# Three of the four pieces of the first x loaded from ScalarE's queue, and eight products of zeros ahead of the first stage

## The chip, the cores and the metric

The kernel runs on one core of a Trainium2 chip. The time is device microseconds of one execution: before the change 606.63 us, the median of 3 runs (606.6 to 607.01).

## The reference

Two layers of a hybrid block over one sequence of 256 tokens, width 1024, all in fp32. Per layer:

- `h = rms_norm(x, g)`, then one projection `h @ w_in` into the parts of three mixers (an mLSTM in chunks of 64, a block attention "MoBA" and a latent attention "MLA").
- MLA takes two latents, `rms_norm(cq, g_cq) @ w_uq` and `rms_norm(ckv, g_ckv) @ w_ukv`, normalises the heads, **rotates** part of queries and keys by `cos` and `sin` of position times frequency, and does causal softmax attention. MoBA rotates its queries and keys as well.
- `x = x + mix @ w_out`, and `x = x + square(relu(rms_norm(x) @ w_up)) @ w_down`.

## The kernel before

Products in fp32 accuracy are made of three passes: `mm3` (L232 to L235) multiplies high by high, high by low and low by high parts. ScalarE makes the high part of a weight piece (`wh`, L207), VectorE the low part (`wl`, L208), up to six pieces ahead of the one TensorE works on. The weights come in order of use as transfers of up to 1 MB on SyncE's queue (`load`, L188), into three rotating buffers `raw`.

The first stage of layer 0 is different, so that it can start early: `do_lat` multiplies the transposed x (`xts`, four pieces of 256 KB, L250) by the first weights (four pieces, L188) in plain fp32 (L547). VectorE scales `xts` in place by the norm's gain (L508) before that, and ScalarE and VectorE split it into `xh` and `xl` (L511, L512) for all later products.

GpSimd makes the tables of cosines and sines for the rotations (`make_trig`, L302 to L342: a chain of some 40 small steps on `tr`, each of which needs the one before; then the tables `tpq`, `tpk`, `tlq`, `tlk`, L421 to L425). The chain starts from the positions (`psi`) and the first 28 columns of the constants (`ck`), both loaded from ScalarE's queue (L246, L247). Outside this chain GpSimd has a few short steps: `gqk` (L629, a product of gains, which reads columns 57 on of the parameters `par`, the second of two transfers, L257), and three casts of the masks and of the identity (L269 to L272), which read the large part of `ck` (L258). VectorE's first use of a table is `rq` (L438, a rotation of MLA's queries).

The order on each engine is set by a scheduler when the kernel is built, from its own estimate of when each step can start; on the chip every engine then takes its list strictly in order. The transfers take eight counters in turn (DMAHW0 to DMAHW7 in the lists below): a transfer is issued only when the one eight places earlier, which had the same counter, has landed.

Of the kernel before, what the change touches and what calls it, by code (L numbers as in the profile page):

```python
# [12 lines left out]
BF16 = mybir.dt.bfloat16  # L13
# [12 lines left out]
DMA_AHEAD = 2  # L26
SPLIT_AHEAD = 6
LAG = 2

ORDERS = [o.split() for o in ("""  # L30
    lat norm q lat lat lat lat q q qout uq uq ukv tables lss p p mla mla qk p p mla mla moba qk rb
# [40 lines left out]
def load_plan(l):  # L72
# [14 lines left out]
    plan = [seq[i:i + 2] for i in range(0, len(seq), 2)]  # L87
    for j in range(16 + LAG):
        if j < 16:
            plan.append([("up", 2 * j), ("up", 2 * j + 1)])  # L90
        if j >= LAG:
            plan.append([("dn", j - LAG)])
    return plan
# [45 lines left out]
def hybrid_kernel(ctx: ExitStack, tc: tile.TileContext, x: bass.AP, xt: bass.AP, pos: bass.AP,  # L139
                  cst: bass.AP, par: bass.AP, wts: bass.AP, out: bass.AP):  # L140
    nc = tc.nc
    V, A, G, T = nc.vector, nc.scalar, nc.gpsimd, nc.tensor
# [7 lines left out]
    def sb(shape, name, dt=F32, bufs=1, tag=None):  # L150
        return tp.tile([128] + list(shape), dt, name=name, tag=tag or name, bufs=bufs)
# [7 lines left out]
    def sm(shape, name):  # L159
        return ps.tile([128] + list(shape), F32, name=name, tag="sm", bufs=4)  # L160
# [74 lines left out]
        T.matmul(o, lh, rl, start=False, stop=stop, **kw)  # L235


    xts = sb([KT, S], "xts", tag="mix")
    warm = cp.tile([128, 1], F32, name="warm")
    G.memset(warm, 0.0)  # L240
# [6 lines left out]
    nc.scalar.dma_start(ck[:, :K_ID], cst[:, :K_ID])  # L247
    first = load(0, 4)
    for k in range(0, KT, 2):
        nc.sync.dma_start(xts[:, k:k + 2], xt[:, k:k + 2])  # L250
        if k == 0:
            nc.sync.dma_start(pr[0][:, :P_CW], par[0, :, :P_CW])
        next(first)
# [246 lines left out]
    for l in range(L):  # L500
# [472 lines left out]

        for j in range(16 + LAG):
            if j < 16:
# [27 lines left out]
                hs[j] = (hh, hlo)  # L1003
            i = j - LAG
            if 0 <= i < SEVEN:
# [99 lines left out]
```

## Time and profile before

| | |
|---|---|
| median of 3 runs | 606.63 us |
| the profiled execution | 606.65 us |
| its span, first to last instruction | 604.9 us |
| TensorE busy | 592.9 us, 98% |
| VectorE busy | 529.3 us, 88% |
| ScalarE busy | 400.9 us, 66% |
| GpSimd busy | 39.7 us, 7% |
| weights and inputs read | 104.71 MB |

Of the span, 1.75 us less than the execution's time, TensorE is idle for 12 us. GpSimd is busy almost only in the first 38 us. In the profile PE is TensorE's products, PEld its weight loads, DVE VectorE, ACT ScalarE, POOL GpSimd and SP SyncE; a step's idle time stands in square brackets with what ended it.

### The profile page before, as it was taken

To read this page: it belongs to the slowest core of one execution; us is meant where nothing else is said; L and a number is where in the kernel's file an instruction comes from. 1 tells how busy PE (TensorE), PEld (TensorE's weight loads), DVE (VectorE), ACT (ScalarE), POOL (GpSimd) and SP (SyncE) were. 2 spreads that over 40 slices of the span, in tenths; PEclk is the share of its full clock that TensorE was granted. 3 is DMA by queue.
4 is the path that set the end of the run, shared out by engine and by line. 5 is a ranking of instruction groups with operands and counts; after the bars stand their busy time and mean duration, and the time that the engine had idled before them with its cause. 6 is when DMAs were issued, how large, how long until landed. Compare 5 with 4: busy or idle time off the path is not lost.

```text
span 604.9 us, 9950 instructions
## 1 busy us (share of the span) xinstructions
PE 592.9 (98%) x3766; PEld 532.5 (88%) x3766; DVE 529.3 (88%) x967; ACT 400.9 (66%) x655; POOL 39.7 (7%) x91
## 2 busy tenths in 40 slices
PE   5999999999999999999999999999999999999997
PEld 4988978889899999989789897888999899999985
DVE  4889886788999999999987997785899999999995
ACT  4776785556776675766766787564676677575770
POOL 7862000000000000000000000000000000000000
PEclk9999999999999999999999999999999999999999
DMA  8785322443554555545637623326446555555521
GB/s 287 292 308 206 134 75 72 168 148 132 209 198 164 202 204 208 201 171 196 244 109 251 237 89 120 106 70 209 139 140 209 186 192 187 202 209 191 196 102 70
DMA packets 17328, 106.39 MB, mean 176 GB/s; under 512 B 2304, under 2 KB 2816, under 8 KB 5504
## 3 DMA queue, kind: packets, MB, share of 16 engines
q1 hardware_dynamic: 16992, 105.75, 50.1%
q8 instruction: 29, 0.48, 0.3%
q14 instruction: 19, 0.16, 0.1%
q10 hardware_dynamic: 288, 0.02, 0.0%
HBM read 104.71 MB, written 1.05 MB: 175 GB/s over the span
## 4 chain that ended last, share of the span: by engine, by line
PE 75%; DVE 14%; POOL 5%; issue 4%; ACT 2%; DVEq 0%; ACTq 0%; POOLq 0%
DVE wl L208 8%; PE up L233 7%; PE up L234 7%; PE up L235 7%; PE P L233 6%; PE P L234 6%; PE P L235 6%; PE acc L235 2%; PE acc L233 2%; PE acc L234 2%; ACT wh L207 1%; PE vp L234 1%; PE op L233 1%; PE vp L233 1%; PE vp L235 1%
## 5 line engine op out<-in xcount | busy, mean ns | idle before, releaser
L208 DVE TENSOR_TENSOR wl<-raw,wh 128x1024 fp32r<-128x1024 f32 (+2 forms) x196 | 217.6, 1129 | 30.6 <-ACT wh L207 26.6
L207 ACT ACTIVATE wh<-raw 128x1024 fp32r<-128x1024 f32 (+2 forms) x196 | 187.5, 979 | 60.6 <-PE acc L234 18.7
L233 PE MATMUL up<-xh,wh 128*128 128x256 f32 x480 | 135.8, 283 | 0.0
L234 PE MATMUL up<-xh,wl 128*128 128x256 f32 x480 | 135.8, 283 | 0.0
L235 PE MATMUL up<-xl,wh 128*128 128x256 f32 x480 | 135.8, 283 | 0.0
L233 PEld LDWEIGHTS up<-xh,wh 128*128 128x128 f32 x480 | 91.9, 192 | 1.5 <-issue 0.4
L234 PEld LDWEIGHTS up<-xh,wl 128*128 128x128 f32 x480 | 92.0, 192 | 1.1
L235 PEld LDWEIGHTS up<-xl,wh 128*128 128x128 f32 x480 | 92.0, 192 | 0.0
L233 PE MATMUL P<-wh,hrh 128*128 128x512 f32 x228 | 89.5, 393 | 0.3 <-DVE xs L970 0.3
L234 PE MATMUL P<-wh,hrl 128*128 128x512 f32 x228 | 89.3, 392 | 0.0
L235 PE MATMUL P<-wl,hrh 128*128 128x512 f32 x228 | 89.0, 390 | 0.0
L208 DVE TENSOR_TENSOR wl<-tsum,wh 128x1024 fp32r<-128x1024 f32 x56 | 66.3, 1222 | 6.1 <-ACT wh L207 6.1
L1001 ACT ACTIVATE hrh<-us 128x896 fp32r<-128x896 f32 (+1 forms) x32 | 29.2, 912 | 56.9 <-DVE us L996 56.8
L207 ACT ACTIVATE wh<-tsum 128x1024 fp32r<-128x1024 f32 x56 | 56.4, 1050 | 14.2 <-DVE tsum L223 14.2
L235 PEld LDWEIGHTS P<-wl,hrh 128*128 128x128 f32 x228 | 42.8, 188 | 9.5
L233 PEld LDWEIGHTS P<-wh,hrh 128*128 128x128 f32 x228 | 42.9, 188 | 9.1 <-DVE xs L970 0.7
L234 PEld LDWEIGHTS P<-wh,hrl 128*128 128x128 f32 x228 | 42.9, 188 | 8.1
L1002 DVE TENSOR_TENSOR hrl<-us,hrh 128x896 fp32r<-128x896 f32 (+1 forms) x32 | 33.2, 1036 | 4.1 <-ACT hrh L1001 4.1
L221 DVE SCALAR_TENSOR_TENSOR tsum<-raw 128x1024 f32<-128x1024 f32 x28 | 34.1, 1218 | 0.0
L991 ACT ACTIVATE rr<-up 128x512 f32<-128x512 f32 x32 | 18.9, 591 | 18.9 <-PE up L235 18.7
L233 PE MATMUL acc<-wh,mh 128*128 128x512 f32 x64 | 25.6, 399 | 0.0
L235 PE MATMUL acc<-wl,mh 128*128 128x512 f32 x64 | 25.0, 390 | 0.0
(366 smaller groups left out, 1100.4 us busy)
## 6 DMA issues: line engine op xcount, KB each, us to landing
raw<-in_wts_dram SPq DMA_DIRECT2D x91, 1024.0 KB, 4.8
raw<-in_wts_dram SPq DMA_DIRECT2D x2, 740.0 KB, 5.9
raw<-in_wts_dram SPq DMA_DIRECT2D x2, 576.0 KB, 5.2
xts<-in_xt_dram SPq DMA_DIRECT2D x4, 256.0 KB, 4.5
raw<-in_wts_dram SPq DMA_DIRECT2D x4, 256.0 KB, 5.2
xs<-in_x_dram SPq DMA_DIRECT2D x1, 1024.0 KB, 10.2
raw<-in_wts_dram SPq DMA_DIRECT2D x2, 512.0 KB, 3.5
raw<-in_wts_dram SPq DMA_DIRECT2D x2, 478.0 KB, 7.3
```

The source lines that it names most:

```text
L207: A.activation(h[:, :n], r, AF.Copy)
L208: V.tensor_sub(lo[:, :n], r, h[:, :n].bitcast(F32))
L221: V.scalar_tensor_tensor(t[:, :1024], r[:, :1024], -1.0, r[:, 512:1536], op0=OP.mult, op1=OP.subtract)
L233: T.matmul(o, lh, rh, start=start, stop=False, **kw)
L234: T.matmul(o, ll, rh, start=False, stop=False, **kw)
L235: T.matmul(o, lh, rl, start=False, stop=stop, **kw)
L991: A.activation(r, up, AF.Relu)
L1001: A.activation(hh, src, AF.Copy)
L1002: V.tensor_sub(hlo, src, hh.bitcast(F32))
```

## The change

Ahead of everything else GpSimd clears a buffer `zero` of 640 bf16 columns, and TensorE multiplies it by itself eight times into a PSUM buffer that nobody reads. The pieces 2 to 4 of `xts` are issued from ScalarE's queue instead of SyncE's. In the changed kernel lines up to L236 stand one number higher, those after it seven.

```diff
+WARM = 8
...
+    zero = sb([640], "zero", BF16, tag="scr", bufs=2)
+    G.memset(zero, 0.0)
+    idle = sm([512], "idle")
+    for i in range(WARM):
+        T.matmul(idle, zero[:, :128], zero[:, 128:], start=i == 0, stop=i == WARM - 1)
     xts = sb([KT, S], "xts", tag="mix")
...
     for k in range(0, KT, 2):
-        nc.sync.dma_start(xts[:, k:k + 2], xt[:, k:k + 2])
+        (nc.scalar if k else nc.sync).dma_start(xts[:, k:k + 2], xt[:, k:k + 2])
         if k == 0:
             nc.sync.dma_start(pr[0][:, :P_CW], par[0, :, :P_CW])
         next(first)
```

The scheduler answers with another order on several engines. GpSimd, from the scaling of the angles by 1/pi (L320, L327 after the change) on. Before:

```order
L320 TENSOR_SCALAR tr<-tr 128x48 [waits Pool_49]
L315 TENSOR_SCALAR tr<-tr 128x48 [waits Pool_49]
L316 TENSOR_TENSOR tr<-tr 128x48 [waits Pool_49]
...
L315 TENSOR_SCALAR tr<-tr 128x96 [waits Pool_49]
L316 TENSOR_TENSOR tr<-tr 128x96 [waits Pool_49]
L629 TENSOR_TENSOR gqk<-par_74 128x2 [waits DMAHW5_49]
...
L332 TENSOR_SCALAR tr<-tr 128x96 [waits Pool_49]
L269 CAST identb<-ck 128x128 [waits DMAHW6_49]
```

And now:

```order
L327 TENSOR_SCALAR tr<-tr 128x48 [waits Pool_49]
L636 TENSOR_TENSOR gqk<-par_85 128x2 [waits DMAHW5_49]
L322 TENSOR_SCALAR tr<-tr 128x48 [waits Pool_49]
L638 MEMSET gqk 16x1 [waits Pool_49] x2
L638 MEMSET gqk 32x1
L323 TENSOR_TENSOR tr<-tr 128x48 [waits Pool_49]
...
L322 TENSOR_SCALAR tr<-tr 128x48 [waits Pool_49]
L276 CAST identb<-ck 128x128 [waits DMAHW6_49]
L278 CAST mk<-ck 128x128
L279 CAST mk<-ck 128x128
L323 TENSOR_TENSOR tr<-tr 128x48 [waits Pool_49]
```

`gqk`, which waits for the second transfer of `par`, stood behind 17 more instructions of the list and now stands right behind the scaling; the casts, which wait for the large part of `ck`, stood some 25 rows behind it and now stand after five more steps of the chain.

SyncE's queue at the start. Before:

```order
L188 DMA raw<-in_wts_dram 128x512 [waits DMAHW2_49]
L188 DMA raw<-in_wts_dram 128x956 [waits DMAHW3_49]
L188 DMA raw<-in_wts_dram 128x956 [waits DMAHW4_49]
L257 DMA par_74<-in_par_dram 128x136 [waits DMAHW5_49]
L258 DMA ck<-in_cst_dram 128x512 [waits DMAHW6_49]
```

And now:

```order
L189 DMA raw<-in_wts_dram 128x512 x3
L189 DMA raw<-in_wts_dram 128x512 [waits DMAHW1_49]
L189 DMA raw<-in_wts_dram 128x956 [waits DMAHW3_49]
L189 DMA raw<-in_wts_dram 128x956 [waits DMAHW4_49]
L264 DMA par_85<-in_par_dram 128x136 [waits DMAHW5_49]
L265 DMA ck<-in_cst_dram 128x512 [waits DMAHW6_49]
```

The first three weight pieces now follow each other; the transfers of `par` and `ck` stand behind the same weights as before. On ScalarE's queue the pieces 2 to 4 of `xts` come behind the first load of `ck`, the third waiting for `psi` to land and the fourth for that part of `ck`. VectorE's list is the same up to `rq`, apart from the place of some 128x2 and 128x256 steps.

## Rows read from the trace of the kernel before

**Rows 1.** The page: busy time, and the chain that ended last.

```profile
PE 592.9 (98%) x3766; PEld 532.5 (88%) x3766; DVE 529.3 (88%) x967; ACT 400.9 (66%) x655; POOL 39.7 (7%) x91
...
PE 75%; DVE 14%; POOL 5%; issue 4%; ACT 2%; DVEq 0%; ACTq 0%; POOLq 0%
```

**Rows 2.** Waits of TensorE, whole span: us in total, times, longest us.

```profile
PE latp L547 <- DVE xts L508: 5.3, 1, 5.3
PE ltp L706 <- DVE lkl L695: 1.2, 1, 1.2
PE qp L235 <- DVE wl L208: 0.8, 1, 0.8
PE P L233 <- DVE xs L970: 0.3, 1, 0.3
```

**Rows 3.** The chain in order of time, 0 to 60 us: start, us, what.

```profile
36.83 0.21 POOL tlqs L424
...
37.30 0.94 DVE ssl L673
...
57.42 0.61 DVE lkl L695
58.08 1.08 PE ltp L706 x8
```

**Rows 4.** GpSimd's instructions in order: start, us, what.

```profile
4.32 0.18 POOL L302 CAST posf<-psi 128x2 f32<-128x2 int32 x1 [1.76 <-DMA psi<-in_pos_dram]
...
5.76 0.50 POOL L320 TENSOR_SCALAR tr<-tr 128x48 f32<-128x48 f32 x1
...
14.03 1.16 POOL L315 TENSOR_SCALAR tr<-tr 128x96 f32<-128x96 f32 x1
...
17.62 0.20 POOL L629 TENSOR_TENSOR gqk<-par 128x2 f32<-128x2 f32 x1
...
23.18 0.45 POOL L332 TENSOR_SCALAR tr<-tr 128x96 f32<-128x96 f32 x1
...
23.71 0.39 POOL L333 TENSOR_TENSOR tr<-tr 128x96 f32<-128x96 f32 x1
...
30.26 1.35 POOL L339 TENSOR_TENSOR tr<-tr 128x96 f32<-128x96 f32 x1
...
36.78 0.24 POOL L424 TENSOR_TENSOR tlqs<-trig,par 128x32 f32<-128x32 f32 x1
```

**Rows 5.** VectorE's instructions in order.

```profile
30.20 2.50 DVE L208 TENSOR_TENSOR wl<-raw,wh 128x1024 fp32r<-128x1024 f32 x2
...
32.99 2.56 DVE L208 TENSOR_TENSOR wl<-raw,wh 128x1024 fp32r<-128x1024 f32 x2
37.06 0.32 DVE L438 TENSOR_TENSOR rq<-lql,tlqs 128x128 f32<-128x128 f32 x1 [1.50 <-POOL tlqs L424]
...
38.29 2.34 DVE L208 TENSOR_TENSOR wl<-raw,wh 128x1024 fp32r<-128x1024 f32 x2
```

**Rows 6.** SyncE's queue: issue of the second transfer of par.

```profile
6.67 0.65 SPq L257 DMA_DIRECT2D par<-in_par_dram  x1
```

**Rows 7.** Transfers issued in the first 12 us: count, KB each, us to landing.

```profile
xts<-in_xt_dram SPq DMA_DIRECT2D x4, 256.0 KB, 4.5
raw<-in_wts_dram SPq DMA_DIRECT2D x4, 256.0 KB, 5.2
...
raw<-in_wts_dram SPq DMA_DIRECT2D x2, 478.0 KB, 7.3
...
par<-in_par_dram SPq DMA_DIRECT2D x1, 68.0 KB, 7.4
```

**Rows 8.** By stretch: PE, PEld, DVE, ACT, POOL busy, clock, DMA share, GB/s.

```profile
12.00:14.00 2.00, 2.00 (x11) 1.61 (x9) 1.59 (x2) 1.40 (x3) 1.77 (x3) 1.00 1.08 431
```

**Rows 9.** TensorE's products into latp by stretch: busy (count), clock, DMA share, GB/s.

```profile
5.29:8.28 2.99, 2.99 (x7) 1.00 0.91 270
8.28:13.58 5.30, 5.30 (x26) 1.00 1.01 381
```

**Rows 10.** TensorE: first product with the low half of the third p piece.

```profile
42.87 0.39 PE L235 MATMUL pp<-wl,xh 128*128 128x512 f32 x1
```

## The prediction

> **What bounds the kernel now.** I read the page first. TensorE is busy 98% of the span and the chain that ended last runs over it for 75%, but GpSimd, busy 7% of the span, holds 5% of that chain [rows 1]. An engine with so little work on the path must sit in one place, so I read where TensorE waits at all: 5.3 us at the start for the first scaled x, 0.8 us for a low half `wl`, and 1.2 us in one wait of the product `ltp` on `lkl` of VectorE [rows 2]. The chain in order of time says what is behind the last: the table `tlqs` on GpSimd until 37.04, then VectorE without a break from 37.30 to 58.03, then TensorE [rows 3]. The lists of the two engines confirm it: VectorE had finished its split at 35.55 and stood 1.50 us before `rq` until GpSimd's `tlqs` was written at 37.02 [rows 4, 5]. So until 58 us the path is not TensorE. It is the chain of GpSimd from the positions (4.32 us) to `tlqs`, and after it a full VectorE. From 58 us on the path is TensorE, which has no wait of over 0.3 us left. Whatever delays `tlqs` therefore delays the end by the same time; whatever makes the first stage earlier ends in the 1.2 us before `ltp`, which become longer.
>
> **The products of zeros.** Clearing `zero` comes first on GpSimd, but GpSimd waited 1.76 us for the positions anyway [rows 4], and half a microsecond of clearing fits in. The eight products are of 512 columns. TensorE's nearest product of 512 columns took 0.39 us [rows 10]; at that duration end to end they take 3.1 us, at twice that 6.3. They may start once the clearing ends, some 1.3 us into the span, and then end between 4.4 and 7.6, against a first stage at 5.29. At the late end they would delay the first stage by 2.3 us, at the early end by nothing; since the durations overlap between neighbours, I take nothing.
>
> They may also make the first stage faster. In it seven products took 2.99 us, 0.427 each, and the next 26 took 5.30, 0.204 each: half the pace and the full one, the levels of 1.2 and 2.4 GHz [rows 9]. The granted clock column reads 1.00 in both, so the pace tells it, not the column. If all ran at the faster pace, the stage would be shorter by 7 x 0.22 = 1.5 us, as far as its data are there. Of that I count nothing: the next products wait for `wl` (0.8 us of [rows 2]), and everything up to 58 us is behind GpSimd.
>
> **The transfers.** SyncE's queue loses three issues, and the weight pieces go out up to a microsecond earlier. The total in front of the second transfer of `par` stays 4 x 256 + 4 x 256 + 2 x 478 KB, with itself 3072 KB or 3.15 MB [rows 7]. Before it was issued at 6.67 and landed 7.4 us later, at 14.07 [rows 6, 7]. At the best pace of the start, 431 GB/s [rows 8], the same bytes take 7.3 us; if they flowed so from 2.5 us on, `par` would land at 9.8. So it lands between 9.8 and 14.07. I take 13.5, near the late end, because the queue held the same bytes at nearly the same times before. The Trainium skill (DMA: Bandwidth & Descriptors, "Issuing engines are not separate DMA queues") says that transfers from several engines run on the same 16 DMA engines and that a second issuer saves only the time of issuing. By that rule the landing stays near 14; a second queue that brought its own bandwidth would move it to 9.8. On ScalarE's queue the third piece of x now waits for the positions (4.3 us), the fourth for the first part of `ck`; behind them stands ScalarE's split of x, which needs these pieces anyway. I count nothing.
>
> **GpSimd's new order.** This is the term that decides. `gqk` stood at 17.62 us and found `par` landed [rows 4]. Now it comes directly behind the scaling that ended at 6.26 (5.76 + 0.50), and it waits for `par` at 13.5. Behind it in the same list stands the whole rest of the chain, which doesn't need `par` until the tables. The casts follow and wait for the large part of `ck`, issued right behind `par`; the five steps and the small clears between them take about 2 us, so that `ck` should have landed by then.
>
> The stall is 13.5 - 6.26 = 7.2 us. Not all of it arrives at `tlqs`, because GpSimd's pace depends on VectorE. A step of 96 columns takes 0.39 to 0.45 us alone and 1.35 us beside VectorE's split [rows 4, 5]. Up to 35.55 VectorE has the same splits as before, so I let GpSimd advance as it did then from 14.03 on: by 35.5 it had done 32 entries of its list, and 32 entries from `gqk` on end in front of the last polynomial steps (L340 now). Twenty remain up to `tlqs`: 12 of the chain at 0.50 us (0.42 with a gap of 0.08), 6.0 us, and 8 of tables at 0.2, 1.6 us. VectorE stands still in that time, so nothing slows them. That gives 35.5 + 7.6 = 43.1 instead of 37.02, 6.1 us later. The bounds: with `par` at 9.8 and the delay passed on unchanged 3.6 us, with 14.07 and passed on in full 7.8 us. I keep 6.1, since the two stretches of rows it rests on are read at both paces.
>
> **What VectorE and TensorE do then.** Behind `rq` in VectorE's list stand two splits that in the profile began at 38.29; everything there moves by 6.1. TensorE runs ahead on split pieces until 42.87, where it needs the `wl` of the first of these two [rows 10], in the profile written at 39.5, now at 45.6: a wait of some 2.7 us. Then it works on to `ltp`, arrives near 59.6 and waits until 58.08 + 6.1 = 64.2, some 4.6 us. The two are 7.3 us in place of 1.2, and the difference is the delay again. No later wait of TensorE is long enough to give any of it back [rows 2].
>
> After such a wait TensorE may start at the slow pace. The wait of 1.2 us was followed by eight `ltp` products in 1.08 us, no sign of slowness [rows 3]; the wait of 5.3 us at the start was followed by 1.5 us of loss [rows 2, 9]. So the bounds are 0 and 1.5 us. The length of 4.6 us is nearer to the latter, but work in pieces between other engines' steps hides part of a slow pace; I take 0.5. The Trainium skill (TensorE: Matmul & The Clock Gate, "What's actually happening") says that the slow level is the default and that activity lifts it, which speaks for the full 1.5 us; by it the sum would be 614.3.
>
> **The sum.** The profiled execution took 606.65 us, 0.02 above the median, so I add to it: 606.65 + 6.1 + 0.5 = 613.2 us.
>
> **The rivals.**
> - *The early `par`.* The steadier queue brings `par` at 9.8 us, and the delay is 3.6 us: 610.2 us. For it: the mean pace from 5.29 to 8.28 was only 270 GB/s [rows 9], so there is room. Against it: the same bytes by the same 16 engines. Chance 0.12.
> - *Nothing on the path.* `par` is there when GpSimd comes to `gqk`, or the delay stays in VectorE's slack; `tlqs` stays at 37.0 and both edits are hidden. The time is 606.6. For it: `gqk` never waited in the profile. Against it: it came 11 us later then, and VectorE had no slack, since it waited for `tlqs` already. It decides only if `par` lands before 6.3. Chance 0.10.
> - *The first stage counts.* The stage that is up to 1.5 us shorter passes its gain to the end, which needs a GpSimd chain that isn't late and a VectorE that is early: 605.3 us, faster than before. For it: TensorE has 98%. Against it: the chain of [rows 3]. Chance 0.05.
> - *All of it.* The delay passes on in full, 7.8 us, and TensorE restarts slowly, 1.5 us: 615.9 us. For it: GpSimd's steps that ran in VectorE's pauses may now meet its splits. Against it: the last third of the chain runs alone. Chance 0.11.
>
> **How the numbers follow.** My forecast, a delay of 5 to 7 us with up to 1.5 us of slow restart, has 0.62, and its own range is 611.5 to 615. The range of 609.3 to 615.5 takes in the early `par` and part of the last rival, and leaves out the cases with no delay and the extreme, 2 in 10. A measurement of this kernel can tell 0.2%, or 1.2 us, from no change. Faster by more than that is the third rival and little of it: 0.05. No change is the second, with 0.09. Slower holds the rest, 0.86.
>
> **What would show it.** GpSimd idle in front of `gqk` for 6 to 8 us, put down to the transfer of `par`; its steps after 35.5 us at 0.4 us each. VectorE's wait at `rq` of some 7.5 us in place of 1.50, until about 43. TensorE waiting at `pp` and for 4 to 5 us at `ltp`, and the rest of the trace the same but later. The first stage at the fast pace from its start, with no gain at 58 us. I am wrong if GpSimd doesn't wait at `gqk`, or if VectorE reaches `rq` late for another reason, or if TensorE gets its pieces through the stall and the end moves by less than the wait at `rq` grew.

## The result, and the profile after

The changed kernel takes 614.51 us (median of 4 runs, 614.34 to 615.05) against 606.77 us (606.6 to 607.01) in the same comparison: ratio 1.0127, 95% interval 1.0112 to 1.0142. It is 7.7 us slower. The profiled execution took 614.35 us with a span of 612.3; before it was 606.65 with 604.9.

The chain of work that ended last tells the story in its first 14 us (start, us, what):

```profile
2.10 4.46 DMA raw<-in_wts_dram
6.57 6.48 DMA par<-in_par_dram
13.12 0.88 POOL gqk L636
14.01 1.36 POOL tr L322
```

The second transfer of `par` is now itself on the path. It was issued at 6.57 and landed 6.48 us later, at 13.05, and GpSimd, with its whole chain of tables behind `gqk`, stood until then. GpSimd's instructions after the change, to be held against [rows 4]; the time in square brackets is the idle time before the step and what ended it:

```profile
4.49 0.18 POOL L309 CAST posf<-psi 128x2 f32<-128x2 int32 x1 [1.36 <-DMA psi<-in_pos_dram]
...
5.93 0.45 POOL L327 TENSOR_SCALAR tr<-tr 128x48 f32<-128x48 f32 x1
13.12 0.88 POOL L636 TENSOR_TENSOR gqk<-par 128x2 f32<-128x2 f32 x1 [6.75 <-DMA par<-in_par_dram]
...
18.63 1.31 POOL L278 CAST mk<-ck 128x128 bf16<-128x128 f32 x1
...
31.52 2.29 POOL L340 TENSOR_TENSOR tr<-tr 128x96 f32<-128x96 f32 x1
...
35.78 1.30 POOL L339 TENSOR_SCALAR tr<-tr 128x96 f32<-128x96 f32 x1
37.17 0.39 POOL L340 TENSOR_TENSOR tr<-tr 128x96 f32<-128x96 f32 x1
...
43.78 0.24 POOL L431 TENSOR_TENSOR tlqs<-trig,par 128x32 f32<-128x32 f32 x1
```

The scaling ends at 6.38, `gqk` begins at 13.12, and `tlqs` at 43.78 instead of 36.78: a stall of 6.75 us has become a delay of 7.0 us. The casts of the masks found `ck` landed and cost no wait, but two of them ran beside a split of VectorE and took 1.3 us each. VectorE, against [rows 5]:

```profile
9.73 0.61 DVE L515 TENSOR_SCALAR xts<-xts,par 128x256 f32<-128x256 f32 x2 [3.17 <-DMA xts<-in_xt_dram]
12.20 0.62 DVE L515 TENSOR_SCALAR xts<-xts,par 128x256 f32<-128x256 f32 x2 [1.86 <-DMA xts<-in_xt_dram]
...
34.22 2.56 DVE L209 TENSOR_TENSOR wl<-raw,wh 128x1024 fp32r<-128x1024 f32 x2 [0.17 <-ACT wh L208]
44.05 0.32 DVE L445 TENSOR_TENSOR rq<-lql,tlqs 128x128 f32<-128x128 f32 x1 [7.27 <-POOL tlqs L431]
```

Two things stand here. The wait in front of `rq` is 7.27 us where it was 1.50, and `rq` begins at 44.05 where it began at 37.06: 6.99 later. And the third and fourth piece of x, scaled at 8.83 and 10.07 before, were scaled at 9.73 and 12.20; with them all of VectorE's splits moved, the last one in front of `rq` from 32.99 to 34.22. The two pieces as they were scaled before, and their issues before:

```profile
8.83 0.82 DVE L508 TENSOR_SCALAR xts<-xts,par 128x256 f32<-128x256 f32 x2 [2.38 <-DMA xts<-in_xt_dram]
10.07 0.62 DVE L508 TENSOR_SCALAR xts<-xts,par 128x256 f32<-128x256 f32 x2 [0.42 <-DMA xts<-in_xt_dram]
...
3.04 0.43 SPq L250 DMA_DIRECT2D xts<-in_xt_dram  x1
4.66 0.43 SPq L250 DMA_DIRECT2D xts<-in_xt_dram  x1
```

In the changed kernel ScalarE's queue issues them at 4.46 and 4.88 (shown as one line), and SyncE's queue the two weight pieces of 478 KB at 4.66 and 5.66:

```profile
4.46 0.82 ACTq L257 DMA_DIRECT2D xts<-in_xt_dram  x2
4.66 0.33 SPq L189 DMA_DIRECT2D raw<-in_wts_dram  x1
5.66 0.33 SPq L189 DMA_DIRECT2D raw<-in_wts_dram  x1
```

TensorE's waits (us in total, times, longest us), against [rows 2]:

```profile
PE pp L236 <- DVE wl L209: 2.1, 1, 2.1
PE latp L554 <- DVE xts L515: 1.9, 3, 0.8
PE ltp L713 <- DVE lkl L702: 1.6, 1, 1.6
PE idle L244 <- POOL warm L247: 1.4, 1, 1.4
PE qkp L234 <- ACT scr L740: 1.4, 1, 1.4
```

and its products where they differ, in order (the products of zeros, the three runs of the first stage, the restart at `pp`, `ltp`):

```profile
1.41 3.60 PE L244 MATMUL idle<-zero 128*128 128x512 bf16 x8 [1.41 <-POOL warm L247]
5.78 3.69 PE L554 MATMUL latp<-xts,raw 128*128 128x256 f32 x16 [0.77 <-DVE xts L515]
10.14 1.99 PE L554 MATMUL latp<-xts,raw 128*128 128x256 f32 x8 [0.67 <-DVE xts L515]
12.61 1.99 PE L554 MATMUL latp<-xts,raw 128*128 128x256 f32 x8 [0.48 <-DVE xts L515]
...
46.54 0.79 PE L236 MATMUL pp<-wl,xh 128*128 128x512 f32 x1 [2.13 <-DVE wl L209]
...
65.12 1.08 PE L713 MATMUL ltp<-ck,lkl 128*96 128x128 f32 x8 [1.60 <-DVE lkl L702]
```

The first stage runs at the fast pace from its first product (16 in 3.69 us, 0.23 each, where [rows 9] had 0.427), and still it ends at 14.6 us, later than the 13.6 at which the next products began before: it waits three times for x. `ltp` begins 7.04 us later than in [rows 3], the first product of the next stage (`vp`) 7.4 us later (71.09 against 63.70), and so it stays to the end. The whole loss is made in the first 71 us. That `tlqs` decides it is seen in VectorE's column by stretch (PE, PEld, DVE, ACT, POOL busy, granted clock, DMA share, GB/s):

```profile
40.00:45.00 5.00, 4.41 (x20) 3.31 (x18) 0.95 (x2) 3.75 (x5) 4.48 (x18) 1.00 0.20 82
45.00:50.00 5.00, 3.46 (x8) 2.74 (x9) 5.00 (x11) 0.00 (x0) 1.69 (x2) 0.66 0.25 51
50.00:55.00 5.00, 3.65 (x17) 2.73 (x16) 5.00 (x19) 2.37 (x4) 1.06 (x3) 1.00 0.96 369
```

VectorE stands still until `rq` and has no gap after it.

### The profile page after: what moved, and what is told of

Its sections match the earlier page's. It is cut to its first block, busy times and chain, and to the rows that moved or that the text cites. A ratio compares the mean times of both kernels' runs of the same rounds, so it can differ in the third digit from the quotient of the medians.

```text
span 612.3 us, 9968 instructions
## 1 busy us (share of the span) xinstructions
PE 598.1 (98%) x3774; PEld 533.4 (87%) x3774; DVE 529.0 (86%) x967; ACT 400.5 (65%) x655; POOL 40.5 (7%) x92
## 4 chain that ended last, share of the span: by engine, by line
PE 79%; DVE 10%; POOL 5%; issue 3%; DMA 2%; ACT 1%; SPq 0%; DVEq 0%; ACTq 0%
PE up L234 8%; PE up L235 8%; PE up L236 8%; PE P L234 7%; PE P L235 7%; PE P L236 7%; DVE wl L209 6%; PE acc L236 2%; PE acc L234 2%; PE acc L235 2%; PE vp L234 1%; PE op L234 1%; PE vp L236 1%; PE op L236 1%; PE vp L235 1%
## 5 line engine op out<-in xcount | busy, mean ns | idle before, releaser
L236 PE MATMUL up<-xl,wh 128*128 128x256 f32 x480 | 135.8, 283 | 0.0
L236 PEld LDWEIGHTS up<-xl,wh 128*128 128x128 f32 x480 | 92.0, 192 | 0.0
L236 PE MATMUL P<-wl,hrh 128*128 128x512 f32 x228 | 89.0, 390 | 0.0
L236 PEld LDWEIGHTS P<-wl,hrh 128*128 128x128 f32 x228 | 42.8, 188 | 9.5
L236 PE MATMUL acc<-wl,mh 128*128 128x512 f32 x64 | 25.0, 390 | 0.0
```

## The experiments

The theory from the two traces was: (1) the order, `gqk` early in GpSimd's list in front of a transfer that lands at 13 us, costs most of the 7.7 us; (2) the late pieces of x cost the rest; (3) the products of zeros neither cost nor bring anything. The rivals were that the second queue costs by itself, and that the order only shows a delay which the late x makes anyway.

**e1: the whole change, with GpSimd's old order.** `gqk` and the casts are tied to steps of the chain where they stood before.

```diff
-            G.tensor_mul(gqk, P[:, P_GC:P_GC + 2], P[:, P_GC + 2:P_GC + 4])
+            with tc.issue_after(step['reduced'].ins) if l == 0 else nullcontext():
+                G.tensor_mul(gqk, P[:, P_GC:P_GC + 2], P[:, P_GC + 2:P_GC + 4])
...
+                with tc.issue_after(step[9].ins):
+                    G.tensor_copy(identb, ident)
```

> The whole change, with GpSimd's old order put back: gqk behind the second reduction of the angles, the casts behind the second step of the polynomial, as in the kernel before. My theory (the loss is GpSimd's stall in front of gqk): no stall, tlqs at 36.5 to 38 us, time 606 to 607.8. Rival A (the transfers on ScalarE's queue cost it, since the third and fourth piece of x land later: VectorE scaled the fourth at 12.20 us in place of 10.07): 611 us or more. Rival B (the products of zeros, their PSUM buffer or TensorE's slow stretch at 46 us): 611 us or more.

Measured: 608.42 us, ratio 1.0028 (1.0019 to 1.0038). VectorE:

```profile
12.09 0.64 DVE L513 TENSOR_SCALAR xts<-xts,par 128x256 f32<-128x256 f32 x2 [1.98 <-DMA xts<-in_xt_dram]
...
37.70 0.32 DVE L443 TENSOR_TENSOR rq<-lql,tlqs 128x128 f32<-128x128 f32 x1 [0.93 <-POOL tlqs L429]
```

Some 6.2 of the 7.7 us are gone with the order alone (608.42 is 1.5 above the 606.90 of the kernel before, run beside it), and `rq` is back at 37.70. It missed its expectation by 0.6 us on the slow side: these 1.5 us are left, with a fourth piece of x as late as in the changed kernel.

**e2: the kernel before, with only the new order.** x and the queues as before, no products of zeros; `gqk` is written right behind the scaling, the casts five steps later.

```diff
+        last = G.tensor_mul(gqk, P[:, P_GC:P_GC + 2], P[:, P_GC + 2:P_GC + 4])
+        for i, c in enumerate((M1, M2, M3)):
+            with tc.issue_after(last.ins):
+                G.tensor_scalar(r1, nq, -c, None, op0=OP.mult)
...
```

> The kernel before with GpSimd's new order alone: gqk directly behind the scaling, the casts five steps of the chain later; transfers as before and no products of zeros. My theory: GpSimd idle for some 7.5 us until par lands at 14.07, tlqs at 44 to 45, time 613.5 to 615. Rivals A and B: 606.6.

Measured: 611.56 us, ratio 1.0081 (1.0066 to 1.0096), below what was expected. GpSimd and VectorE:

```profile
13.36 0.76 POOL L319 TENSOR_TENSOR gqk<-par 128x2 f32<-128x2 f32 x1 [7.30 <-DMA par<-in_par_dram]
...
34.33 1.30 POOL L342 TENSOR_SCALAR tr<-tr 128x96 f32<-128x96 f32 x1
...
32.77 2.56 DVE L208 TENSOR_TENSOR wl<-raw,wh 128x1024 fp32r<-128x1024 f32 x2
41.59 0.32 DVE L448 TENSOR_TENSOR rq<-lql,tlqs 128x128 f32<-128x128 f32 x1 [6.27 <-POOL tlqs L434]
```

The order alone makes the stall, 7.30 us, even longer than in the changed kernel, but only 4.5 us of it reach `rq` (41.59 against 37.06). GpSimd made up 2.8 us. The difference to the changed kernel lies in VectorE's splits: with x on time the last split in front of `rq` ended at 35.33 (36.78 in the changed kernel), and GpSimd, whose steps are slow beside them, was then in the 35th entry of its list from `gqk` on; in the changed kernel it was in the 33rd when the split ended, 1.45 us later. The casts are part of it: all three took 0.29 us each here, and two of them 1.3 us each in the changed kernel.

**e3: the products of zeros alone.**

```diff
+    zero = sb([640], "zero", BF16, tag="scr", bufs=2)
+    G.memset(zero, 0.0)
+    idle = sm([512], "idle")
+    for i in range(WARM):
+        T.matmul(idle, zero[:, :128], zero[:, 128:], start=i == 0, stop=i == WARM - 1)
```

> The kernel before with the products of zeros alone; all of x on SyncE's queue. In the list that the scheduler makes gqk stands 15 instructions behind the scaling, nearly as before, so my theory: no stall of over 1 us, time 606 to 607.5, the first stage up to 1.5 us shorter without effect on the end. Rival B: 611 us or more. Rival A: 606.6.

Measured: 606.80 us, ratio 0.9996 (0.9986 to 1.0005), as expected. TensorE:

```profile
1.41 3.59 PE L243 MATMUL idle<-zero 128*128 128x512 bf16 x8 [1.41 <-POOL warm L246]
5.32 6.04 PE L553 MATMUL latp<-xts,raw 128*128 128x256 f32 x24 [0.32 <-DVE xts L514]
11.81 1.97 PE L553 MATMUL latp<-xts,raw 128*128 128x256 f32 x8 [0.45 <-DVE xl L518]
```

The products end before the first piece of x is scaled, and the stage ends at 13.78 because its data do; `tlqs` is where it was (`rq` at 36.90).

**e4: the queue alone.**

```diff
-        nc.sync.dma_start(xts[:, k:k + 2], xt[:, k:k + 2])
+        (nc.scalar if k else nc.sync).dma_start(xts[:, k:k + 2], xt[:, k:k + 2])
```

> The kernel before with x on ScalarE's queue alone. The scheduler puts gqk three chain steps behind the scaling and the casts five steps after that, so my theory: GpSimd stalls some 5 to 6 us in front of gqk and the time is 612 to 614.5. Rival A gives the same time, but without the stall; rival B: 606.6.

Measured: 614.22 us, ratio 1.0123 (1.0106 to 1.014), as expected: 7.3 us of loss, nearly the 7.7 of the whole change. The scheduler's list isn't quite that of the changed kernel (`gqk` stands three steps of the chain further back, `rq` nine instructions further back in VectorE's list, four of them splits), but the stall is the same kind:

```profile
13.05 0.19 POOL L629 TENSOR_TENSOR gqk<-par 128x2 f32<-128x2 f32 x1 [5.52 <-DMA par<-in_par_dram]
...
10.22 0.62 DVE L508 TENSOR_SCALAR xts<-xts,par 128x256 f32<-128x256 f32 x2
...
59.82 1.94 PE L706 MATMUL ltp<-ck,lkl 128*96 128x128 f32 x8 [4.21 <-DVE lkl L695]
```

So one edited line of transfers makes the new order of GpSimd's list, without the products of zeros. The loss isn't made up in the same way, though: `rq` begins at 45.04, TensorE waits 4.21 us at `ltp` and is slow after it, and the fourth piece of x is scaled at 10.22, almost as early as before, although it was issued when the changed kernel issues it (4.78 against 4.88). What differs ahead of it is that the two large weight pieces went out at 6.03 and 6.40 here, behind it. The shares of these parts in the 7.3 us weren't followed.

**e5 and e6: the transfers instead of the order.** Both are the changed kernel with `gqk` and the casts tied early as in e2, and bring their data earlier. The edit shown is that of e6. In e5 the second transfer of `par` goes out ahead of the weights; in e6 the large part of `ck` as well.

```diff
             nc.sync.dma_start(pr[0][:, :P_CW], par[0, :, :P_CW])
+            nc.sync.dma_start(pr[0][:, P_CW:], par[0, :, P_CW:])
+            nc.sync.dma_start(ck[:, K_ID:], cst[:, K_ID:])
```

> The whole change with GpSimd's new order kept, and the second transfer of par issued third on SyncE's queue, ahead of the weights. My theory (GpSimd's list stands behind the transfer that its front entry needs): no stall at gqk, but one at the casts, which GpSimd reaches near 9.2 us and for which the large part of ck lands near 13.7: 4 to 5 us of stall, rq near 42, time 611 to 613. Rival (the order itself costs, not the transfer it waits for): 614.5 as the change.

> As e5, with the large part of ck moved ahead of the weights too, so that neither entry waits long although both stand early in GpSimd's list. My theory: GpSimd idle under 1 us at either, tlqs near 37.5 to 38.5; the first weights come 0.8 us later because 324 KB stand in front of them; time 608 to 609.5, as e1 (608.42) or up to 1 us above. Rival: 614.5.

Measured: e5 611.86 us, ratio 1.0092 (1.0076 to 1.0108), as expected. The stall only moves to the next step whose data are late, the first cast (waits of GpSimd):

```profile
POOL identb L334 <- DMA ck<-in_cst_dram: 4.5, 1, 4.5
...
POOL gqk L326 <- DMA par<-in_par_dram: 0.5, 1, 0.5
```

e6: 611.55 us, ratio 1.0086 (1.0071 to 1.0102), 2 us above its expectation. GpSimd waits for nothing but 0.4 us, and `rq` begins at 38.14, so this is another loss. TensorE now waits for its weights at the start and for 2.4 us at `ltp`, and is slow after both (its products, then the stretches):

```profile
7.24 7.11 PE L564 MATMUL latp<-xts,raw 128*128 128x256 f32 x24 [2.23 <-DMA raw<-in_wts_dram]
...
59.53 1.94 PE L724 MATMUL ltp<-ck,lkl 128*96 128x128 f32 x8 [2.40 <-DVE lkl L713]
```

```profile
8.00:10.00 2.00, 2.00 (x7) 1.57 (x6) 0.00 (x0) 0.00 (x0) 1.75 (x8) 0.57 0.75 209
...
60.00:62.00 2.00, 2.00 (x11) 1.83 (x10) 1.69 (x7) 1.08 (x2) 0.00 (x0) 0.50 0.00 0
```

The granted clock of 0.50 is the lower level, 1.2 of 2.4 GHz; the eight `ltp` products took 1.94 us instead of 1.08. 324 KB put ahead of the first weights gave time to GpSimd and took some from the first stage, whose first product begins at 7.24 instead of 5.78. How the rest of e6's 4.8 us is made up wasn't followed: its lists differ on VectorE and TensorE too.

**e7 and e8: the order that the chain asks for.** Kernel before with `gqk` and the casts behind all tables, and MLA's tables ahead of MoBA's; all of x on SyncE's queue. e7 has the products of zeros, e8 hasn't.

```diff
+            with tc.issue_after(step['tables'].ins) if l == 0 else nullcontext():
+                G.tensor_mul(gqk, P[:, P_GC:P_GC + 2], P[:, P_GC + 2:P_GC + 4])
...
+                with tc.issue_after(step['tables'].ins):
+                    G.tensor_copy(identb, ident)
```

> Towards a better version: the kernel before with the products of zeros, gqk and the casts behind all tables, and the tables of the MLA rotation ahead of those of MoBA. My theory (up to 58 us the path is GpSimd's chain): 1.2 us of small steps and 0.8 us of MoBA's tables leave the chain, tlqs near 35 us, VectorE no longer waits at rq, TensorE's wait at ltp (0.6 us in e3) goes, and with the faster first stage the time is 604.5 to 605.8. Rival (TensorE sets the time also up to 58 us): 606.8, as e3.

> As e7 without the products of zeros. My theory: TensorE's wait of 1.2 us at ltp goes, the first stage stays at its slow start: 605.3 to 606. If the products of zeros bring anything once GpSimd is off the path, e7 is below this by 0.5 to 1.3 us; if not, they are equal.

Measured: e7 605.39 us, ratio 0.9981 (0.9971 to 0.9991), as expected: 1.3 us better than the kernel before, and the best version here. Its two moves (`gqk` and the casts behind the tables, MLA's tables ahead of MoBA's) weren't run one by one. e8 606.16 us, ratio 0.9995 (0.9984 to 1.0006), slightly above its expectation. In e7 VectorE and TensorE have:

```profile
35.41 0.32 DVE L442 TENSOR_TENSOR rq<-lql,tlqs 128x128 f32<-128x128 f32 x1 [0.60 <-POOL tlqs L428]
```

```profile
PE ltp L717 <- DVE lkl L706: 0.3, 1, 0.3
```

`rq` begins 1.65 us earlier than in [rows 5], and of the 1.2 us at `ltp` 0.3 are left: TensorE has become the bound. Between e7 and e8 lie 0.77 us, 0.13%, which is less than can be told apart here (the two ranges of runs overlap); that the zeros pay once the chain is out of the way is likely, not shown.

**e9 and e10: only the second piece of x on ScalarE's queue.** e9 is e1 with the third and fourth piece back on SyncE's queue, ahead of the large weights; e10 is e7 with the same.

```diff
-        (nc.scalar if k else nc.sync).dma_start(xts[:, k:k + 2], xt[:, k:k + 2])
+        (nc.scalar if k == 2 else nc.sync).dma_start(xts[:, k:k + 2], xt[:, k:k + 2])
```

> As the changed kernel with GpSimd's old order, but only the second piece of x is on ScalarE's queue; the third and fourth are back on SyncE's, ahead of the large weights. Theory (the 1.5 us left over with GpSimd's old order come from the late third and fourth piece of x): the fourth piece is scaled near 10.1 us instead of 12.09, the first stage ends about 1 us earlier, and the time is 606.3 to 607.0 us. Rival (the 1.5 us come with a second queue as such, or with VectorE's list that the edit leaves): the time stays at 608 to 608.6 us.

> The kernel with the tables ahead of gqk and the casts, the products of zeros, and only the second piece of x on ScalarE's queue. Theory: x isn't late, so that this piece changes nothing: 605.0 to 605.7 us. Rival (a second queue as such costs 1.5 us): 606.5 to 607.2 us.

Measured: e9 606.67 us, ratio 0.9996 (0.9988 to 1.0005), as expected. VectorE and TensorE in e9:

```profile
9.59 0.70 DVE L513 TENSOR_SCALAR xts<-xts,par 128x256 f32<-128x256 f32 x2 [1.91 <-DMA xts<-in_xt_dram]
```

```profile
11.48 1.97 PE L552 MATMUL latp<-xts,raw 128*128 128x256 f32 x8 [0.24 <-DVE xl L517]
```

The last piece is scaled at 9.59 instead of 12.09, the first stage ends at 13.45, and the 1.5 us of e1 are gone. So a second queue as such doesn't cost them, and with the two pieces back on time they go. Not all of them need be the pieces' own, since the lists differ between e1 and e9, which the edit can't avoid: `ltp` begins 0.94 us earlier in e9 (58.21 against 59.15), and another 0.67 us lie behind it, where TensorE's list has three `qkp` products in front of the first `vp` in e9 and eight in e1. How much each would cost alone isn't shown. e10 took 605.97 us, ratio 0.9985 (0.9976 to 0.9995), 0.3 above its expectation and, each held against the kernel before, not told apart from e7: the second queue brings nothing on top of the right order.

## Why the prediction was right, point by point

The forecast was 613.2 us, slower, and its mechanism is the one that decided. e1 and e2 show it from both sides: without the order the loss falls to 1.5 us, and the order alone costs 4.7 us (611.56 against the 606.9 of the kernel before).

- *The landing of `par`.* Taken 13.5, measured 13.05, between the bounds. The early `par` of the first rival did not come: the bytes in front of it stayed the same. The Trainium skill's sentence that issuing from another engine adds no DMA engines (DMA: Bandwidth & Descriptors, "Issuing engines are not separate DMA queues") agrees with it: with two queues 422 GB/s flowed from 10 to 15 us, with one 416.
- *The stall.* Taken 7.2, measured 6.75, since the scaling ended at 6.38 and `par` came 0.45 earlier.
- *What arrives at `tlqs`.* Taken 6.1, measured 7.0. The form of the working holds: when VectorE's splits ended, 32 entries of the list from `gqk` on were done and the 33rd was running, as taken. What was wrong is the sentence that VectorE has the same splits up to 35.55: they ended at 36.78, as they did in e1 with its late x, and at 35.33 in e2 and 35.60 in e3 with x on time. The 33rd entry, which the working didn't count, ended at 37.08, and the twenty behind it ran in 6.9 us (37.08 to 44.02) where 7.6 were taken. So the start of the lone part was taken 1.6 us too early and its length 0.7 us too long, and that 6.1 came near is in part luck. e2 shows 4.5 instead of 7.0: its splits ended 1.45 us earlier, with two entries fewer left.
- *The transfers of x: "I count nothing."* This is the step that failed, in a prediction whose main mechanism holds. The third piece was issued at 4.46 on ScalarE's queue, behind the wait for the positions, where SyncE had issued it at 3.04. The fourth went out some 0.2 us later than before, but now behind the first of the two weight pieces of 478 KB (4.88 against 4.66), both of which had followed it on one queue; it was scaled 2.1 us later. e4, where both went out behind it and it was scaled at 10.22, speaks for these pieces as the cause. Price: up to 1.5 us by itself (e1 against the kernel before; e9 gives them back), and some 2.5 us more at `rq` together with the order (6.99 against 4.53 in e2). The two together, 1.5 + 4.7 = 6.2, are less than the 7.7 us of the change for that reason.
- *TensorE's waits.* Taken 2.7 at `pp` and 4.6 at `ltp`; measured 2.13 and 1.60, with 1.35 at `qkp`. The missing time is in the first stage, 1.2 us late, and in the slow restart.
- *The slow restart.* Taken 0.5 behind `ltp`. It came behind `pp`: the granted clock was 0.66 from 45 to 50 us, and seven products took 3.16 us (46.54 to 49.70) where at the fast pace of 0.23 they take 1.6. It cost nothing at the end, since VectorE was busy through all of that time and `ltp` waited for VectorE. Behind `ltp` the eight products took 1.08 us as before. That clock agrees with the sentence of the Trainium skill (TensorE: Matmul & The Clock Gate, "What's actually happening") that the slow level is the default and activity lifts it, but the 1.5 us that it would have added to the sum were not on the path: that its 614.3 lies beside the measured 614.35 is chance.
- *What the sum had not.* Between `ltp` and the first `vp` TensorE has eight `qkp` products instead of five in its list, 5.97 us instead of 5.62; in e1 it is 5.97 as well. And 0.3 us lie outside the span (614.35 - 612.3 against 606.65 - 604.9). With these, 6.99 at `rq`, 0.05 more up to `ltp`, 0.35 and 0.3 make the 7.7 us. The 0.5 for a restart stood in the sum for something else and came out nearly right by chance.
- *The products of zeros.* Taken as nothing, and e3 shows nothing. The faster first stage ends in waits for x. The pace of 0.204 read from [rows 9] is a little too fast, since its two stretches count 33 products where the stage has 32; the changed kernel has 0.23, so that the gain held possible was 1.4 us and not 1.5.
- *The rivals.* "Nothing on the path" fell with the 6.75 us at `gqk`, "the first stage counts" with e3. "All of it" was half right: the stall passed on in full (6.75 became 7.0), for its reason, steps of GpSimd that met VectorE's splits; the slow restart did not.

## What to carry to other kernels

An edit that moves a few transfers can change the list of an engine that it doesn't touch: with a scheduler, compare the order of every engine, and look for a short step that waits for a late transfer and has a long chain behind it in the same list. Repair it where it is, by placing that step behind the chain (e1, e7); bringing its data earlier (e5, e6) moved the wait to the next step or took the transfers' time from somebody else. Before splitting loads over two queues, ask what the one queue's order protected: here it kept the smaller, urgent pieces ahead of the large ones.

## What the runs showed of the hardware that was not expected

- A piece of x on a second queue landed later, not sooner: the fourth, issued at about the same time, was scaled at 12.20 us and not at 10.07, while the DMA engines together moved 422 GB/s. This came with a large transfer issued ahead of it on the other queue (4.66 against 4.88); in e4, where the large ones went out behind it, it was scaled at 10.22.
- After a wait of 2.13 us at `pp` TensorE restarted at the slow pace (clock 0.54 from 48 to 50 us in the changed kernel), and after one of 2.40 us in e6 and one of 4.21 us in e4 as well (there eight `ltp` products took 1.94 us); after the waits of 1.60 us in the changed kernel and 1.2 us before [rows 2, 3] the eight `ltp` products took 1.08 us, without a loss. The prediction had feared this only of the long wait.
- GpSimd's step of 96 columns, 0.39 us alone, took up to 2.29 us beside VectorE's splits, so a shift of these splits can cost GpSimd more than the shift: against e2 they ended 1.45 us later and `rq` began 2.5 us later.
